# Fixing the TensorE order of seven block products, and holding a set of sums behind the last split before them

## The chip, the cores and the metric

The kernel runs on one core of one Trainium2 chip. The metric is the device time in microseconds from start to end of one execution. Matmuls run on TensorE (PE), loads of their stationary operand are shown as PEld. VectorE (DVE), ScalarE (ACT), GpSimd (POOL) and SyncE (SP, which issues most DMAs) work beside it. Each engine works off its own queue in a fixed order, and engines wait for each other by semaphores.

## The reference

One layer of a sequence model with 1024 frames and width 1024, in float32: a norm, one wide projection, three parallel mixers, a gated sum of their outputs, an output projection with a residual, and then the part that matters here:

```
u = causal_dwconv(rmsnorm(x, norm2_g[l]) @ w_up[l], ffn_conv_w[l], ffn_conv_b[l])
u_g, u_v = jnp.split(u, 2, axis=-1)
x = x + (jax.nn.silu(u_g) * u_v) @ w_down[l]
return rmsnorm(x, final_g)
```

`w_up` is 1024 x 5632, that is 44 blocks of 128 output channels, two blocks (gate and value) for each of 22 channel groups f. The convolution has three taps along the frames.

## The kernel before, in words

Activations are kept with channels on the partitions and frames along the free axis, in two halves of 512 frames. Every float32 operand is split into a rounded part and a rest ("hi" by a ScalarE cast, L99, "lo" by a VectorE subtraction, L100), and a product takes three matmuls for each 128 rows of contraction: hi by hi, hi by lo, lo by hi.

**The plain blocks.** The second norm (`norm`, L867) scales the eight row tiles of each half of the frames in place in `x2`, on VectorE (L874), and splits each into `p_hi` and `p_lo`. The first half of the frames is normalised during the output projection, the second half inside `up_end` (L895), while TensorE works on the first two blocks of `w_up`. `up_end` is a `manual_schedule` block for PE, DVE and ACT: there the instructions of the block keep their written order on each of the three engines, while instructions from outside the block may still be put between them. Groups f = 0, 1, 2 (`up_begin`, `up_end`, `up_plain`) are computed as six plain products of 48 matmuls, each into a two-bank PSUM tile `ps_g`, of which there are two. `up_conv` (L883, by `conv`, L577) reads such a tile: one ACT instruction (L581) and two taps on DVE (L585). The tile is free for another product when the second tap has read it.

**The pairs.** For f = 3 to 21, the two blocks of a group and the two halves of the frames form a 2 x 2 block product, which `pair_gemm` (L173) does with seven half-size products instead of eight, each of twelve matmuls over 512 columns. Their left operands are the weight `wa` (first block), and `s12`, `s34`, `qb`, made from both blocks in `operands` (L142) by four in-place sums on DVE (L159) and by splits. The `operands` instructions are traced with `high_priority(offset=200)`. Of the tiles `w_b` (for `qb`) and `w_s` (for `s12` and `s34`) there is room for one pair; of `wa` for two. The third sum of L159 overwrites the raw block that `qb` is split from. Their right operands are three quarters of the normalised input, b11, b21, b22, and four sums of quarters, t1 to t4, which `sums` (L206) makes once, in place in `x2`: eight DVE subtractions (L214), each followed by a split (a cast and an L100 subtraction, tile `t`).

The seven products, as written, with x and y the two banks of one `ps_g` tile, z and v banks of their own (`ps_m`):

- P1: wa by b11 into x; ACT copies x away (u0, L188)
- P2: wa by b21 into y; DVE adds y and u0 (L183, first half of the first result c)
- P3: s12 by t2, accumulated on x; ACT copies x away (u1)
- P4: s12 by t1 into z; DVE adds z to u1
- P5: s34 by t3, accumulated on x; ACT copies x away (u2); DVE adds z and u2
- P6: s34 by b22 into v; DVE adds v and u1 (second half of the first result c)
- P7: qb by t4, accumulated on x; ACT copies x (L204, second result c)

Both results then go through `up_conv`, a Silu (L919), a product (L920) and a store to DRAM (L219).

**What sets the order.** Outside `manual_schedule` blocks, a planner in the compiler orders each engine's queue ahead of time from its own estimate of durations: among what it holds to be ready it takes the instruction of the best priority, which is the earlier one in the program, where `high_priority(offset=200)` counts as 200 instructions earlier. The products of `pair_gemm` lie in no such block, nor does `sums`.

Of the kernel before, what the change touches and what calls it, by code (L numbers as in the profile page):

```python
# [9 lines left out]
F32 = mybir.dt.float32  # L10
# [3 lines left out]
ALU = mybir.AluOpType  # L14
# [8 lines left out]
HALF = 512  # L23
# [24 lines left out]
class Trunk:  # L48
# [48 lines left out]

    def split(self, hi, lo, src, eng=None):
        self.nc.scalar.copy(out=hi, in_=src)  # L99
        (eng or self.nc.vector).tensor_tensor(out=lo, in0=src, in1=hi.bitcast(F32), op=ALU.subtract)  # L100

    def weight(self, src, dst=None):
        with self.tc.high_priority(offset=200):
# [69 lines left out]
    def pair_gemm(self, pool, srcs, outs):  # L173

        nc = self.nc
        wa, s12, s34, qb = self.operands(pool, srcs)
        b11, b21, b22, t1, t2, t3, t4 = self.bs
        ps = self.pg.tile([P, T], F32, name="ps_g")
        x, y = ps[:, 0:HALF], ps[:, HALF:]
        z, v = (self.pm.tile([P, HALF], F32, name="ps_m") for _ in range(2))  # L180
        oa, ob = outs
        tmp = lambda: pool.tile([P, HALF], F32, name="u", bufs=4)
        add = lambda out, p, q: nc.vector.tensor_tensor(out=out, in0=p, in1=q, op=ALU.add)  # L183
        u = []

        def keep():
            u.append(tmp())
            nc.scalar.copy(out=u[-1], in_=x)  # L188

        self.product(wa, 0, b11, x)  # L190
        keep()
        self.product(wa, HALF, b21, y)
        add(oa[:, 0:HALF], y, u[0])
        self.product(s12, HALF, t2, x, start=False)
        keep()
        self.product(s12, 0, t1, z)
        add(u[1], z, u[1])
        self.product(s34, 0, t3, x, start=False)
        keep()
        add(ob[:, HALF:], z, u[2])  # L200
        self.product(s34, HALF, b22, v)
        add(oa[:, HALF:], v, u[1])
        self.product(qb, 0, t4, x, start=False)
        nc.scalar.copy(out=ob[:, 0:HALF], in_=x)  # L204

    def sums(self, pool, xs):  # L206

        (x11, x21), (x12, x22) = [[x[:, ks] for ks in (slice(0, KT // 2), slice(KT // 2, KT))] for x in xs]
        new = lambda: [pool.tile([P, KT // 2, HALF], F32R, name="t", align_bytes=ALIGN, bufs=8) for _ in range(2)]
        t4, t1, t2, t3 = (new() for _ in range(4))  # L210
        for to, out, p, q in ((t1, x11, x12, x11), (t3, x12, x22, x12), (t2, x22, x22, x11), (t4, x21, x21, x22)):
            for k in range(0, KT // 2, 2):
                ks = slice(k, k + 2)
                self.nc.vector.tensor_tensor(out=out[:, ks], in0=p[:, ks], in1=q[:, ks], op=ALU.subtract)  # L214
                self.split(to[0][:, ks], to[1][:, ks], out[:, ks])
        return [[[t[part][:, k] for k in range(KT // 2)] for part in range(2)] for t in (t1, t2, t3, t4)]
# [886 lines left out]
def build(tc, ins, outs, dbg=None):  # L1103
    stages = dbg or dict(hg=8, ml=4, mb=4, rest=True)
    left = dict(side="left", reuse_waits="tile")
    right = dict(side="right", reuse_waits="tile")
    with ExitStack() as ctx:
        t = Trunk(tc, ctx, ins, outs, dbg)
        t.y_dram = [outs[f"y{i}"] for i in range(3)] if dbg else [
            t.dr.tile([KT, P, T], F32, name=f"y_dram{i}") for i in range(3)]  # L1110
        t.x2_d = t.dr.tile([KT, P, T], F32, name="x2_dram")
        t.act_d = t.dr.tile([22, P, T], F32, name="act_dram")
        with tc.tile_pool(name="gp", bufs=3, **right) as t.gp:
            with tc.tile_pool(name="hp", bufs=1, **right) as hp:
                with ExitStack() as ms:
                    late = ms.enter_context(tc.tile_pool(name="late", bufs=1, **right))
                    early = lambda: Mix(ms.enter_context(tc.tile_pool(name="early", bufs=1, **right)), late)
                    mp, begun, v = t.first(hp, early)
                    t.late_consts(late)
                    t.hg_setup()  # L1120
                    for hd in range(stages["hg"]):
                        if hd and hd % 2 == 0:
                            v = t.hg_v(mp, hd // 2)
                        t.hg_head(mp, hd, v, begun if hd == 0 else None)
                        if hd == 5:
                            t.scalars(mp)
                    for hd in range(stages["ml"]):
                        t.ml_head(mp, hd)
                    for g in range(stages["mb"]):
                        t.mb_group(mp, g)  # L1130
                if not stages["rest"]:
                    return
                yp = ctx.enter_context(tc.tile_pool(name="yp", bufs=KT, **left))
                xps = ExitStack()
                xp = xps.enter_context(tc.tile_pool(name="x2", bufs=2, **left))
                br = t.branches(yp, xp)
                mixed = next(br)
            with tc.tile_pool(name="mx", bufs=KT, **right) as mxp:
                mix = [t.pair(mxp, mixed[j]) for j in range(KT - 2)]
                for _ in br:  # L1140
                    pass
                mix += [t.pair(mxp, mixed[j]) for j in range(KT - 2, KT)]
                x2 = [xp.tile([P, KT, HALF], F32, name="x2") for _ in range(2)]

                hs = [[[], []] for _ in range(4)]
                for n, part, e in itertools.product((1, 0, 2, 3), range(2), ("p_hi", "p_lo")):
                    w = yp.tile([P, T], F32R, name=e, align_bytes=ALIGN, bufs=KT)
                    hs[n][e == "p_lo"] += [w[:, 0:HALF], w[:, HALF:]]
                place = lambda part, kt, hf: hs[kt // 4 * 2 + hf][part][kt % 4]
                rhs = lambda part, kt, ts: place(part, kt, ts.start // HALF)  # L1150
                tmp = t.halves_of(lambda: t.gp.tile([P, T], F32, name="gate", bufs=3))
                src = [lambda kt, hf=hf: x2[hf][:, kt] for hf in range(2)]
                sums = lambda hf: t.norm_sums(tmp, src[hf], slice(0, HALF))

                def norm2(dg, hf):
                    t.norm(src[hf], dg, src[hf], "norm2_g",
                           lambda kt, a: t.split(place(0, kt, hf), place(1, kt, hf), a))
                t.out_proj(mix, x2, 0, range(KT))
                t.out_proj(mix, x2, 1, [0])
                dg = sums(0)  # L1160
                t.out_proj(mix, x2, 1, [1])
                norm2(dg, 0)
                t.out_proj(mix, x2, 1, range(2, KT))
            begun = t.up_begin(rhs)
            dg = sums(1)
            with tc.tile_pool(name="tp", bufs=1, **right) as tp:
                ws = t.up_end(*begun, lambda: norm2(dg, 1))
                t.up_plain(range(1, PLAIN), rhs, ws)
                t.bs = [hs[0], hs[2], hs[3]] + t.sums(tp, x2)
                xps.close()  # L1170
                with tc.tile_pool(name="a1", bufs=1, **left) as pool:
                    t.up_pairs(pool, range(PLAIN, 22))
            with tc.tile_pool(name="dn", bufs=1, **right) as pool:
                t.down(yp, pool)
# [15 lines left out]
```

## Time and profile before

| what | value |
|---|---|
| median of 3 runs | 2552.4 us (2552.34 to 2555.36) |
| profiled execution, device time | 2553.12 us |
| its span | 2551.4 us |
| PE busy | 2498.3 us, 98% of the span, 13076 matmuls |
| DVE busy | 1427.4 us, 56% |
| ACT busy | 963.0 us, 38% |
| mean granted clock of TensorE | 0.992 of full speed |

The device time of the profiled execution is 1.7 us longer than its span. Busy shares are over the whole span; a busy PE counts a pipelined matmul from its start to its modelled end (389 ns), although the next starts about 227 ns after it, so gaps have to be read from the starts. Times in rows are microseconds from the start of the span.

### The profile page before, as it was taken

Reading aid. Unit: us, or ns where it says so; the run is one execution under the profiler, and the core shown is the slowest. Engines: PE = TensorE matmul, PEld = TensorE weight load, DVE = VectorE, ACT = ScalarE, POOL = GpSimd, SP = SyncE. Lnnn points to the kernel's source line nnn. Section 1 sums busy time; section 2 is a strip of 40 time slices with the busy share of each in tenths; the row PEclk is TensorE's granted clock in tenths of the full one; section 3 lists DMA queues with packets and bytes.
Section 4 is the critical chain, followed back from the end, with each engine's and each line's share of the span. In section 5 each row is a group of like instructions: output and inputs, shape, how many; then the busy total and the mean of one; then the engine's idle time right before and its main releaser. Section 6 shows DMA issues by size and latency. Waiting matters only on the chain.

```text
span 2551.4 us, 30921 instructions
## 1 busy us (share of the span) xinstructions
PE 2498.3 (98%) x13076; PEld 2135.3 (84%) x13076; DVE 1427.4 (56%) x1792; ACT 963.0 (38%) x1177; POOL 42.1 (2%) x73
## 2 busy tenths in 40 slices
PE   8999999999999999999999999999989999999998
PEld 7898989898899899899888888888777777778886
DVE  6576767773344466675412223234766777775445
ACT  5444444553343346355312112122334444451212
POOL 1000000000000000000000000000000000000000
PEclk8999999999999999999999999999999999999999
DMA  4111111111121122212312213115211222244321
GB/s 148 34 42 42 42 42 38 58 50 58 67 75 66 43 83 83 76 54 86 124 50 93 73 48 111 48 63 172 95 66 58 85 88 75 75 142 152 111 75 66
DMA packets 56363, 195.06 MB, mean 76 GB/s; under 512 B 6536, under 2 KB 7176, under 8 KB 56224
## 3 DMA queue, kind: packets, MB, share of 16 engines
q1 hardware_dynamic: 48320, 164.77, 19.5%
q0 software_dynamic: 7904, 28.32, 2.8%
q8 instruction: 103, 1.69, 0.3%
q14 instruction: 36, 0.29, 0.0%
HBM read 160.45 MB, written 32.60 MB: 76 GB/s over the span
## 4 chain that ended last, share of the span: by engine, by line
PE 94%; DVE 3%; ACT 1%; DMA 1%; issue 1%; DVEq 0%; SPq 0%; ACTq 0%
PE ps_g L136 54%; PE ps_g L170 10%; PE ps_g L251 10%; PE ps_m L136 5%; PE ps_m L170 4%; PE ps_m L444 3%; PE ps_m L776 1%; PE ps_m L251 1%; PE ps_m L453 1%; PE ps_m L687 1%; PE ps_m L658 1%; PE ps_m L463 1%; PE ps_m L416 0%; PE ps_m L638 0%; PE ps_m L660 0%
## 5 line engine op out<-in xcount | busy, mean ns | idle before, releaser
L136 PE MATMUL ps_g<-h,w_hi 128*128 128x512 f32 x2592 | 721.6, 396 | 3.5 <-DVE h L100 2.0
L136 PEld LDWEIGHTS ps_g<-h,w_hi 128*128 128x128 f32 x2592 | 484.4, 188 | 103.4 <-ACT h L99 3.1
L99 ACT CAST w_hi<-w_raw 128x1024 fp32r<-128x1024 f32 x190 | 198.6, 1046 | 845.0 <-PE ps_g L136 722.6
L100 DVE TENSOR_TENSOR w_lo<-w_raw,w_hi 128x1024 fp32r<-128x1024 f32 x190 | 232.5, 1224 | 335.7 <-ACT w_hi L99 335.3
L136 PE MATMUL ps_g<-h,w_lo 128*128 128x512 f32 x1296 | 411.0, 394 | 0.0
L136 PEld LDWEIGHTS ps_g<-h,w_lo 128*128 128x128 f32 x1296 | 243.7, 188 | 50.4
L251 PE MATMUL ps_g<-w_hi,h 128*128 128x256 f32 x1408 | 261.1, 284 | 0.0
L136 PE MATMUL ps_g<-p_hi,w_hi 128*128 128x512 f32 x768 | 241.9, 393 | 8.7 <-DVE gate L585 6.6
L136 PE MATMUL ps_g<-p_lo,w_hi 128*128 128x512 f32 x768 | 241.3, 392 | 2.8 <-DVE p_lo L100 2.5
L136 PE MATMUL ps_g<-p_hi,w_lo 128*128 128x512 f32 x768 | 240.7, 391 | 0.0
L251 PEld LDWEIGHTS ps_g<-w_hi,h 128*128 128x128 f32 x1408 | 221.3, 192 | 0.6
L251 PE MATMUL ps_g<-w_lo,h 128*128 128x256 f32 x704 | 200.1, 284 | 0.0
L136 PEld LDWEIGHTS ps_g<-p_hi,w_hi 128*128 128x128 f32 x768 | 145.1, 189 | 40.6 <-ACT t L99 7.0
L136 PEld LDWEIGHTS ps_g<-p_lo,w_hi 128*128 128x128 f32 x768 | 145.2, 189 | 35.3 <-DVE p_lo L100 4.8
L136 PEld LDWEIGHTS ps_g<-p_hi,w_lo 128*128 128x128 f32 x768 | 145.1, 189 | 30.1
L251 PEld LDWEIGHTS ps_g<-w_lo,h 128*128 128x128 f32 x704 | 134.9, 192 | 0.5
L170 PE MATMUL ps_g<-t,w_s 128*128 128x512 f32 x456 | 113.3, 391 | 1.9 <-DVE w_s L100 1.2
L585 DVE SCALAR_TENSOR_TENSOR gate<-c,c_vec,gate 128x1023 f32<-128x1023 f32 x76 | 97.2, 1279 | 25.0 <-ACT gate L581 25.0
L170 PEld LDWEIGHTS ps_g<-t,w_s 128*128 128x128 f32 x456 | 85.4, 188 | 21.2 <-DVE w_s L100 1.6
L962 DVE TENSOR_TENSOR x<-ps_g,x 128x1024 f32<-128x1024 f32 x40 | 49.0, 1225 | 91.3 <-PE ps_g L136 86.9
L840 DVE TENSOR_TENSOR gate<-ps_g,gate 128x1024 f32<-128x1024 f32 x16 | 19.6, 1225 | 123.4 <-PE ps_g L136 123.4
L99 ACT CAST p_hi<-w_raw 128x1024 fp32r<-128x1024 f32 x48 | 50.1, 1048 | 92.3 <-DMA w_raw<-act_dram 33.6
(292 smaller groups left out, 3531.5 us busy)
## 6 DMA issues: line engine op xcount, KB each, us to landing
w_raw<-w_up SPq DMA_DIRECT2D x44, 512.0 KB, 3.5
w_raw<-w_hg SPq DMA_DIRECT2D x24, 512.0 KB, 3.4
w_raw<-w_v SPq DMA_DIRECT2D x24, 512.0 KB, 3.4
ta<-rows SPq DMA_DIRECT2D x24, 512.0 KB, 4.3
w_raw<-w_gate SPq DMA_DIRECT2D x24, 512.0 KB, 3.4
w_raw<-w_br SPq DMA_DIRECT2D x24, 512.0 KB, 3.5
w_raw<-y_dram SPq DMA_DIRECT2D x24, 512.0 KB, 3.5
act_dram<-gate POOLq DMA_DIRECT2D x22, 512.0 KB, 3.2
```

Of the source, the lines that this page charges most:

```text
L99: self.nc.scalar.copy(out=hi, in_=src)
L100: (eng or self.nc.vector).tensor_tensor(out=lo, in0=src, in1=hi.bitcast(F32), op=ALU.subtract)
L136: self.nc.tensor.matmul(out=out, lhsT=w[:, ks], rhs=rhs(part, kt, ts), start=kt == 0 and w is hi and part == 0, stop=kt == kts - 1 and w i ...
L170: self.nc.tensor.matmul(out=out, lhsT=w[x][:, ks], rhs=b[y][k], start=start and k == i == 0, stop=stop and k == 3 and i == 2, skip_group_c ...
L251: self.nc.tensor.matmul(out=out, lhsT=self.h[hf][part][:, 4 * i + k, o:o + P], rhs=w[:, ks], start=start and k == 0 and w is hi and part = ...
L444: nc.tensor.matmul(out=pa[0:m, c], lhsT=z[:, c * P:c * P + m], rhs=part(1)[:, c], start=True, stop=True)
L453: nc.tensor.matmul(out=pa[:, j], lhsT=c3(k)[:, c + j], rhs=qs[:, c + j], start=True, stop=True)
L463: nc.tensor.matmul(out=po[:, j], lhsT=A[:, c], rhs=v[:, c, vs], start=True, stop=c == 0)
L585: nc.vector.scalar_tensor_tensor(out=out[:, a:ts.stop], in0=ps[:, a - d:ts.stop - d], scalar=w(d), in1=out[:, a:ts.stop], op0=ALU.mult, op ...
L658: nc.tensor.matmul(out=po, lhsT=A[:, c], rhs=v[:, c], start=True, stop=c == 0)
L687: nc.tensor.transpose(out=pt[:, j], in_=src(4 * hf + j), identity=self.ident)
L962: nc.vector.tensor_tensor(out=x2[j], in0=ps, in1=x2[j], op=ALU.add)
```

## The change

Two edits. In `pair_gemm`, the seven products and what stands between them move into a new method `seven`, called inside a `manual_schedule` block for TensorE alone: the 84 matmuls of a pair keep their written order, P1 to P7, on TensorE. The other engines, and the order of one pair's matmuls against another pair's, stay with the planner. And `sums` is traced under `issue_after`, which queues each of its DVE instructions behind the last `lo` subtraction of the second norm on that engine's queue; it adds no wait.

```diff
     def split(self, hi, lo, src, eng=None):
         self.nc.scalar.copy(out=hi, in_=src)
-        (eng or self.nc.vector).tensor_tensor(out=lo, in0=src, in1=hi.bitcast(F32), op=ALU.subtract)
+        return (eng or self.nc.vector).tensor_tensor(out=lo, in0=src, in1=hi.bitcast(F32), op=ALU.subtract)
...
+        with self.tc.manual_schedule(engines={mybir.EngineType.PE}):
+            self.seven(wa, s12, s34, qb, (x, y, z, v), u, keep, add, oa, ob)
+        nc.scalar.copy(out=ob[:, 0:HALF], in_=x)
+
+    def seven(self, wa, s12, s34, qb, banks, u, keep, add, oa, ob):
+        b11, b21, b22, t1, t2, t3, t4 = self.bs
+        x, y, z, v = banks
         self.product(wa, 0, b11, x)
         keep()
         self.product(wa, HALF, b21, y)
...
         self.product(qb, 0, t4, x, start=False)
-        nc.scalar.copy(out=ob[:, 0:HALF], in_=x)
...
+                done = []
+
                 def norm2(dg, hf):
                     t.norm(src[hf], dg, src[hf], "norm2_g",
-                           lambda kt, a: t.split(place(0, kt, hf), place(1, kt, hf), a))
+                           lambda kt, a: done.append(t.split(place(0, kt, hf), place(1, kt, hf), a)))
...
-                t.bs = [hs[0], hs[2], hs[3]] + t.sums(tp, x2)
+                with tc.issue_after(done[-1].ins):
+                    t.bs = [hs[0], hs[2], hs[3]] + t.sums(tp, x2)
```

## Rows read from the trace of the kernel before

**Rows 1.** The page's chain of work that ended last, by engine.
```profile
PE 94%; DVE 3%; ACT 1%; DMA 1%; issue 1%; DVEq 0%; SPq 0%; ACTq 0%
```

**Rows 2.** Windows: PE, PEld, DVE, ACT, POOL busy, granted clock, DMA share, GB/s.
```profile
2000.00:2100.00 100.00, 96.63 (x421) 78.31 (x420) 76.57 (x86) 46.23 (x55) 2.65 (x5) 1.00 0.23 78
```

**Rows 3.** Waits of PE, 1830 to 2300: us in total, times, longest.
```profile
PE ps_g L170 <- ACT u L188: 14.6, 20, 1.8
PE ps_g L136 <- DVE gate L585: 6.6, 1, 6.6
PE ps_g L136 <- DVE p_lo L100: 2.5, 2, 1.9
```

**Rows 4.** Timeline of PE over one pair: start, us, line, tiles, count, idle before.
```profile
1988.04 3.01 PE L170 MATMUL ps_g<-t,w_b 128*128 128x512 f32 x12 [0.68 <-ACT u L188]
1990.89 0.39 PE L170 MATMUL ps_g<-p_hi,w_hi 128*128 128x512 f32 x1
...
1993.61 0.39 PE L170 MATMUL ps_g<-p_hi,w_hi 128*128 128x512 f32 x1
...
1996.33 0.61 PE L170 MATMUL ps_g<-t,w_s 128*128 128x512 f32 x2
...
1997.69 2.47 PE L170 MATMUL ps_g<-t,w_s 128*128 128x512 f32 x10
...
2004.53 2.88 PE L170 MATMUL ps_g<-t,w_s 128*128 128x512 f32 x12
2008.09 3.02 PE L170 MATMUL ps_g<-t,w_b 128*128 128x512 f32 x12 [0.68 <-ACT u L188]
```

**Rows 5.** Line 170, 1994.53 to 1994.60: the semaphore instruction on PE's queue.
```profile
L170 PEldq EVENT_SEMAPHORE  x1: 51/51/51, 1994.5 to 1994.5; - x1
```

**Rows 6.** Timeline of DVE over the same pair.
```profile
1987.05 1.28 DVE L585 SCALAR_TENSOR_TENSOR gate<-c,c_vec,gate 128x1023 f32<-128x1023 f32 x1 [1.32 <-ACT gate L581]
...
1991.83 0.69 DVE L100 TENSOR_TENSOR w_b<-w_raw,w_b 128x512 fp32r<-128x512 f32 x1 [1.70 <-ACT w_b L99]
1992.55 0.69 DVE L159 TENSOR_TENSOR w_raw<-w_raw 128x512 f32<-128x512 f32 x1
1993.81 0.69 DVE L183 TENSOR_TENSOR c<-ps_g,u 128x512 f32<-128x512 f32 x1 [0.56 <-PE ps_g L170]
...
1995.01 1.28 DVE L585 SCALAR_TENSOR_TENSOR gate<-c,c_vec,gate 128x1023 f32<-128x1023 f32 x1
1996.21 2.35 DVE L100 TENSOR_TENSOR w_s<-w_raw,w_s 128x1024 fp32r<-128x1024 f32 x2
```

**Rows 7.** Timeline of ACT over the same pair.
```profile
1987.40 1.07 ACT L188 COPY u<-ps_g 128x512 f32<-128x512 f32 x2 [0.38 <-PE ps_g L170]
...
1991.19 0.60 ACT L99 CAST w_b<-w_raw 128x512 fp32r<-128x512 f32 x1
...
1993.46 1.03 ACT L99 CAST w_s<-w_raw 128x1024 fp32r<-128x1024 f32 x1
```

**Rows 8.** Timeline of PE in the last part of the second norm.
```profile
1838.17 0.50 PE L136 MATMUL ps_g<-p_lo,w_hi 128*128 128x512 f32 x1 [1.90 <-DVE p_lo L100]
...
1860.72 1.19 PE L136 MATMUL ps_g<-p_hi,w_hi 128*128 128x512 f32 x2 [6.56 <-DVE gate L585]
```

**Rows 9.** Timeline of DVE in the same stretch.
```profile
1836.30 1.22 DVE L214 TENSOR_TENSOR x<-x,x 128x1024 f32<-128x1024 f32 x1
1837.44 0.68 DVE L100 TENSOR_TENSOR p_lo<-x,p_hi 128x512 fp32r<-128x512 f32 x1
...
1850.62 0.69 DVE L100 TENSOR_TENSOR p_lo<-x,p_hi 128x512 fp32r<-128x512 f32 x1
...
1856.89 0.75 DVE L585 SCALAR_TENSOR_TENSOR gate<-ps_g,c_vec,gate 128x512 f32<-128x512 f32 x1
...
1859.82 0.75 DVE L585 SCALAR_TENSOR_TENSOR gate<-ps_g,c_vec,gate 128x512 f32<-128x512 f32 x1
```

**Rows 10.** The window behind that wait, with PE's granted clock.
```profile
1861.00:1867.00 6.00, 6.00 (x16) 4.66 (x16) 6.00 (x6) 1.99 (x2) 0.00 (x0) 0.54 0.28 87
```

More of the change, by code (lines that the diff above doesn't have):

```diff
@@ L176, in pair_gemm @@
         wa, s12, s34, qb = self.operands(pool, srcs)
-        b11, b21, b22, t1, t2, t3, t4 = self.bs
         ps = self.pg.tile([P, T], F32, name="ps_g")
```

## The prediction, made before the changed kernel ran

> **What bounds the kernel now.** I read the page's chain first: TensorE holds 94% of what ended last [rows 1], so a change pays only where it closes a gap between matmuls or opens one. The windows of the pair stage show PE busy for 96.63 of 100 us at clock 1.00, with DVE at 76.57 and ACT at 46.23 [rows 2]. The list of PE's waits then names the gaps: 20 times an ACT copy of u, and once each, in the stretch ahead of the pairs, the conv taps (6.6 us) and, 2.5 us in all, the lo parts of the norm [rows 3]. Last, the timelines. Over one pair [rows 4] they show the order that the planner chose: P7 of pair A (from 1988.04), P2 of pair B (1990.89), P1 of pair C (1993.61), two matmuls of P3 of B (1996.33), five of P4 and P6 as filling, the ten others of P3 (1997.69), P4 and P6, P5 (2004.53), a wait for u2, and P7 (2008.09). That the first twelve of 1990.89 are P2 is read from DVE, which adds y and u0 at 1993.81, right behind them [rows 6].
>
> **Part 1, the order of the seven products: what goes.** A pair takes 2008.09 - 1988.04 = 20.05 us [rows 4]. Matmuls follow each other by (1993.61 - 1990.89) / 12 = 0.227 us, so 84 of them take 19.04 us, and 1.0 us a pair is lost. Nearly all of it lies behind P5: its twelve matmuls from 2004.53 would let P7 start at 2007.25, and it starts at 2008.09, 0.84 later, with about 0.1 more in the first steps after the wait (its twelve take 3.02 us where P5's take 2.88). I count 0.95 a wait. In the written order P6, 12 x 0.227 = 2.72 us, stands between P5 and P7, and the copy, about 0.6 us long (1.07 for two) [rows 7], lies beneath it. The wait goes, 20 times [rows 3]: 19.0 us at most from this alone.
>
> **What may come: two more reads of the same tile.** At 1994.5 PE's queue works off a semaphore instruction [rows 5], directly after DVE's addition of y and u0 ends (1993.81 + 0.69 = 1994.50) [rows 6]. P3 writes x, and the addition reads y, the other bank of the same tile; I read this as P3 waiting for that addition, and take it that P2 waits in the same way for the copy u0. Today P1 of the next pair hides the first, and u0 was copied before P7 (the second of the two copies at 1987.40) [rows 7]. If a pair ran by itself in the written order, each place would cost about what the copy costs today, 0.95, and 0.99 + 0.11 = 1.1 for the addition (its end against P2's last start plus a step, 1994.60 - 1993.61). The edit does not tie one pair to the next, so P1 of the next pair, 2.72 us, can stand there as it does today. I take nothing for these two; the other end is 2.05 us a pair.
>
> By the Trainium skill, "PSUM — Partial Sum Buffer", section "PSUM bank collisions raise a hardware error", a semaphore has to guard PSUM by bank and quadrant, so a reader of y need not hold up a writer of x, and these two places would cost nothing in any order. The semaphore behind the addition says otherwise here. By the rule the gain would be 19.0 us whatever the planner interleaves; by the row it needs the next pair as cover.
>
> **The chain behind P7.** There is room for one pair's `w_b`, so after P7 of A come, one after another: the cast of `w_b` (1991.19), its lo (1991.83), the third sum of L159 (1992.55), the cast of `s12` (1993.46), its lo (1996.21, the first of two that take 2.35 together, so done at about 1997.4) [rows 6, 7]. Counted from 1990.89, the lo is there after 6.5 us. The third matmul of P3 needs it. Today it starts after 6.8 us, because five matmuls of P4 and P6 were put ahead. In the written order it comes after 24 + 2 matmuls, 5.9 us. So with DVE's queue unchanged PE would wait 0.6 us, and with 0.1 each for the semaphore and the restart lose 0.85 of the 0.95 again. Two things in the chain can give way: DVE waits 0.56 us for y ahead of the addition, and then runs a conv tap of 1.2 us ahead of the lo [rows 6]. Without the tap it is there after 5.3 us, with neither after 4.8, and nothing is lost. But the written order also moves P6 behind P5, and with it the first result's two taps (today before P7, 1987.05) [rows 6] into this very window: 2 x 1.2 = 2.4 us more on DVE.
>
> I choose no loss, since these operand instructions carry priority over the taps and addition, and a tap that starts before them costs at most its 1.2 us: a lo due at 4.8, plus one such, is 6.0, all but on time. The ends are a gain of 0.95 and a loss of 1.45 a pair (below). The first pair has no cover yet and may pay at the two reads what it saves, so I count 18 of the 20 waits: 18 x 0.95 = 17.1 us.
>
> **Part 2, the sums behind the last split.** They remain 16 DVE instructions, with their ACT casts. Today six of them, four L214 and two t, lie between 1836.30 and the last p_lo at 1850.62 [rows 9]; one takes 1837.44 - 1836.30 = 1.14 us of the queue. The first delays the first p_lo, on which PE sits idle for 1.90 us [rows 8]. Moving them brings the last p_lo forward by 6 x 1.14 = 6.8 us. The lo waits of 2.5 us [rows 3] go, but that alone ends nothing: PE next needs a free `ps_g`, which the second tap frees, and waits 6.56 us for it, until 1860.72 [rows 8]. The first tap stands at 1856.89, five sum instructions behind the last p_lo, the second at 1859.82, two further on [rows 9]. If the planner leaves five sums ahead of the first tap again, both taps and PE's restart move 6.8 us forward. If it places the taps by PE's progress, the six merely go elsewhere ahead of them, and the gain is 0. At best all goes: 6.6 + 2.5, and the half-speed stretch after the wait, 16 matmuls in 6 us at clock 0.54 [rows 10] where 6 / 0.227 = 26 fit, 10 x 0.227 = 2.3 us: 11.4. I take 6.8, the reading by the row of the tap. The lo of the next weight and the Silu lie behind the taps as now; the sums' first reader is a product of the first pair, behind two whole plain groups, so that later sums cost nothing.
>
> **The sum.** 17.1 + 6.8 = 23.9 us off the profiled execution's 2553.1: 2529.2. The median lies 0.7 below that execution: **2528.5 us**.
>
> **Rivals.** (1) The wait moves to the lo of s12, at equal price. For it: the 6.5 against 5.9 us above, and a DVE at 77% whose queue is fixed ahead. Against: the order of DVE is planned anew. Part 1 then gives (0.95 - 0.85) x 19 = 2 us, with part 2 2543.6; without part 2, 2550, no change.
>
> The Trainium skill's "Perfetto Trace Analysis", section "Optimization Strategy", says that a gap that repeats can mean too little memory for the next tile. Here the repeating gap ends with a copy, yet `w_b` for one pair is what this rival hangs on; by that rule, order alone would not remove it.
>
> (2) The other side: the chain behind P7 becomes the bound. Three taps of the two results stand ahead of the lo on DVE. From the end of w_b's cast, 0.9 us behind P7, DVE then works without a break, its short instructions (0.69 busy, less the overlap of some 0.08 that 1.22 busy and 1.14 apart show [rows 9]) 0.6 each: three taps 3.6, w_b lo 0.6, L159 twice 1.2, the addition 0.6, the lo 1.2: 8.1 us. PE waits 8.1 - 5.9 + 0.2 = 2.4 a pair in place of 0.95; 19 x 1.45 = 27.5 us more. With part 2 that is 2573, without 2580. It decides from the point where the lo comes later than 5.9 + 0.95 - 0.2 = 6.65 us behind P7. For it: 2.4 us move into a window that has some 0.1 to spare; against: the priority of the operands. Pairs without cover would come out at the same: 2.05 - 0.95 = 1.1 a pair, 21 us.
>
> (3) The planner keeps what matters as it was, taps and filling: 2552.
>
> **How the numbers follow.** Forecast 0.44; rival 1 0.20; rival 2 0.30; rival 3 0.06. The forecast's own range is 2517 (19.0 + 11.4, and the odd longer waits) to 2537 (15, no part 2). Under 0.2%, 5 us, nothing can be told from no change. Faster: 0.44 and 0.11 of rival 1, 0.55. Same: 0.09 of rival 1, 0.04 of rival 3, 0.02 of a mild rival 2, 0.15. Slower 0.30. The range that holds 8 in 10 has to reach rival 2: 2518 to 2574.
>
> **What would show it.** Right: no wait for u in the list; 84 matmuls from P7 to P7 in 19.0 to 19.2 us; P1 of the next pair between P2 and P3; the lo of s12 under 5.9 us behind P7; no L214 ahead of the last p_lo, and PE's restart near 1854. Wrong in part 1: waits for DVE `w_s` (rivals 1, 2), or for ACT u at P2 and DVE c at P3 (no cover). Wrong in part 2: the taps still near 1857 and a wait for them longer than 6.6 us.

## The result, and the profile after

The changed kernel takes **2583.91 us** (median of 4 runs, 2583.8 to 2587.7) where the kernel before took 2552.56 beside it: ratio **1.0124, 95% interval 1.0106 to 1.0141**, 31 us slower. The forecast was 2528.5 us. It lies 11 us above what the second rival gave (2573) and 10 above the end of the range.

The page's chain by engine, where TensorE has fallen from 94% [rows 1] and DVE risen from 3%:

```profile
PE 88%; DVE 8%; ACT 1%; issue 1%; DMA 1%; DVEq 0%; SPq 0%; ACTq 0%
```

The same window as [rows 2], and two windows of 4 us; columns as there. DVE and ACT do less in the same time, because the pairs come more slowly. The clock column, which was 1.00 in every window of the pairs before, falls to 0.97, and to 0.57 and 0.59 in the short windows:

```profile
2000.00:2100.00 100.00, 92.45 (x390) 74.90 (x389) 66.70 (x76) 41.73 (x51) 2.66 (x5) 0.97 0.23 76
...
1976.00:1980.00 4.00, 4.00 (x12) 3.11 (x12) 1.23 (x2) 1.38 (x2) 0.53 (x1) 0.57 0.91 282
2020.00:2024.00 4.00, 4.00 (x12) 3.15 (x11) 1.38 (x2) 1.43 (x2) 0.53 (x1) 0.59 0.92 267
```

PE's waits, 1820 to 2340, against [rows 3]. The 20 waits for a copy of u are gone but for one; in their place stand 18 for the lo of `s12`, 17 of them of 1.89 us and the last pair's of 3.4:

```profile
PE ps_g L170 <- DVE w_s L100: 35.5, 18, 3.4
PE ps_g L136 <- DVE gate L590: 6.8, 1, 6.8
PE ps_g L170 <- DVE w_lo L100: 2.6, 1, 2.6
...
PE ps_g L136 <- DVE p_lo L100: 0.8, 1, 0.8
PE ps_g L170 <- ACT u L187: 0.7, 1, 0.7
```

PE over one pair (P7, P2's first, P1 of the next pair's first, P3, P3 again), answering [rows 4]:

```profile
2052.61 2.88 PE L170 MATMUL ps_g<-t,w_b 128*128 128x512 f32 x12
2055.33 0.39 PE L170 MATMUL ps_g<-p_hi,w_hi 128*128 128x512 f32 x1
...
2058.05 0.39 PE L170 MATMUL ps_g<-p_hi,w_hi 128*128 128x512 f32 x1
...
2060.77 0.62 PE L170 MATMUL ps_g<-t,w_s 128*128 128x512 f32 x2
...
2063.27 2.56 PE L170 MATMUL ps_g<-t,w_s 128*128 128x512 f32 x10 [1.89 <-DVE w_s L100]
```

P7 follows P6 with no wait, and P1 of the next pair stands between P2 and P3, both as forecast. The third matmul of P3 starts at 2063.27, 2.5 us behind the first. DVE and then ACT in the same pair show why (against [rows 6, 7]):

```profile
2054.82 1.28 DVE L590 SCALAR_TENSOR_TENSOR gate<-c,c_vec,gate 128x1023 f32<-128x1023 f32 x1 [1.31 <-ACT gate L586]
2056.02 0.68 DVE L100 TENSOR_TENSOR w_b<-w_raw,w_b 128x512 fp32r<-128x512 f32 x1
2056.62 1.27 DVE L590 SCALAR_TENSOR_TENSOR gate<-c,c_vec,gate 128x1022 f32<-128x1022 f32 x1
2057.81 0.68 DVE L159 TENSOR_TENSOR w_raw<-w_raw 128x512 f32<-128x512 f32 x1
2058.42 1.27 DVE L590 SCALAR_TENSOR_TENSOR gate<-c,c_vec,gate 128x1023 f32<-128x1023 f32 x1
2059.61 0.68 DVE L182 TENSOR_TENSOR c<-ps_g,u 128x512 f32<-128x512 f32 x1
2060.21 0.68 DVE L159 TENSOR_TENSOR w_raw<-w_raw 128x512 f32<-128x512 f32 x1
2060.81 1.27 DVE L590 SCALAR_TENSOR_TENSOR gate<-c,c_vec,gate 128x1022 f32<-128x1022 f32 x1
2062.00 2.35 DVE L100 TENSOR_TENSOR w_s<-w_raw,w_s 128x1024 fp32r<-128x1024 f32 x2
```

```profile
2055.30 0.62 ACT L99 CAST w_b<-w_raw 128x512 fp32r<-128x512 f32 x1 [0.52 <-PE ps_g L170]
...
2057.93 1.06 ACT L924 ACTIVATE gate<-gate 128x1024 f32<-128x1024 f32 x1 [0.24 <-DVE gate L590]
2058.90 1.04 ACT L99 CAST w_s<-w_raw 128x1024 fp32r<-128x1024 f32 x1
```

All four taps stand ahead of the lo of `s12`. The second holds up the third sum of L159 by its 1.2 us, and on ACT a Silu (L924) holds up the cast by another 0.4 (the sum ends at 2058.49, the cast starts at 2058.90), so that the cast ends only at 2059.94; and then an addition, a sum and the last tap go first, so that the lo starts at 2062.00. It is the first of the two instructions in that row and ends near 2063.2, 7.9 us behind P7's end at 2055.33.

The starts of consecutive matmuls give the account of the pair stage (first matmul of the first pair to the first plain product behind the last pair; the 1608 steps between would take 364.2 us at 0.2265 each). "Waits" is the sum of gaps beyond a step that are over 0.3 us, "half speed" that of steps of 0.35 to 0.53 us:

| kernel | stage, us | waits | half speed |
|---|---|---|---|
| before | 388.6 | 20.6 | 0 |
| both edits | 424.4 | 44.0 | 12.3 |

23.4 us are longer waits and 12.3 us are matmuls at the 1.2 GHz level, 0.43 us apart, about eight of them in seven of the pairs and at the stage's end. Part 2 gives back 5.2: the first pair starts at 1901.82 where it started at 1907.07 (1901.95 with the sums alone, `e2` below). 35.8 - 5.2 = 30.6 is the difference of the spans (2582.0 - 2551.4).

### The profile page after: what moved, and what is told of

Its sections match the earlier page's. It is cut to its first block, busy times and chain, and to the rows that moved or that the text cites. A ratio compares the mean times of both kernels' runs of the same rounds, so it can differ in the third digit from the quotient of the medians.

```text
span 2582.0 us, 30945 instructions
## 1 busy us (share of the span) xinstructions
PE 2508.1 (97%) x13076; PEld 2146.0 (83%) x13076; DVE 1424.5 (55%) x1792; ACT 964.1 (37%) x1177; POOL 42.1 (2%) x73
## 4 chain that ended last, share of the span: by engine, by line
PE 88%; DVE 8%; ACT 1%; issue 1%; DMA 1%; DVEq 0%; SPq 0%; ACTq 0%
PE ps_g L136 53%; PE ps_g L256 9%; PE ps_m L136 5%; PE ps_g L170 4%; PE ps_m L170 4%; DVE gate L590 3%; PE ps_m L449 3%; PE ps_m L781 1%; PE ps_m L256 1%; DVE c L182 1%; ACT gate L586 1%; PE ps_m L458 1%; DVE w_s L100 1%; PE ps_m L692 1%; PE ps_m L663 1%
## 5 line engine op out<-in xcount | busy, mean ns | idle before, releaser
L170 PE MATMUL ps_g<-t,w_s 128*128 128x512 f32 x456 | 124.6, 420 | 38.1 <-DVE w_s L100 35.5
```

The source lines that it names most:

```text
L170: self.nc.tensor.matmul(out=out, lhsT=w[x][:, ks], rhs=b[y][k], start=start and k == i == 0, stop=stop and k == 3 and i == 2, skip_group_c ...
```

## The experiments

Each was timed in several executions beside the kernel before, unless said otherwise. The line numbers in their rows can differ by one from those of the changed kernel.

**Each part alone.** `e1` drops the `issue_after`, `e2` the `manual_schedule`.

> Only the written order of the seven products; the sums stay where they were. Theory (the whole loss lies in the pairs: each waits some 2.1 us for the lo of s12, and half of them run eight matmuls at the lower clock): the pairs cost what they cost with both edits, 22.05 us each, and the 5.3 us that the sums brought are lacking: 2589 us. Rival (moving the sums puts DVE's queue out of step, and the order itself gains what was forecast): 2535 us, with 19.1 us a pair and no wait for w_s.

> Only the sums behind the last split; the planner is free to order the products. Theory: the wait for the second tap ends some 4.4 us earlier and the pairs begin 5.3 us earlier, nothing else changes: 2547 us, 20.05 us a pair, a wait for the copy u2 in each pair. Rival (the moved sums are what disturbs the pairs): 2575 us or more. Rival (the sums' gain appears only where the pairs wait less): 2552 us.

```diff
 # e1
-                with tc.issue_after(done[-1].ins):
-                    t.bs = ...
+                t.bs = ...
 # e2
-        with self.tc.manual_schedule(engines={mybir.EngineType.PE}):
+        if True:
             self.seven(...)
```

The order alone: **2585.48 us, ratio 1.0128 (1.0113 to 1.0144)**. The sums alone: **2548.68, 0.9983 (0.9974 to 0.9993)**. So the loss is the order's, and the sums do what was meant, at a little over half the forecast's size. With the order, the sums bring 1.6 us, not 3.9, a difference within the spread of these runs (2583.8 to 2587.7 and 2584.25 to 2587.92). The two profiled executions show where such a difference can come from: the order alone starts its pairs 4.0 us later than both edits, but its stage takes 420.7 us with waits of 40.2, against 424.4 and 44.0.

**Cutting the chain: room for two pairs' `w_b`.**

> Both edits, and room for the w_b of two pairs; for the memory the copies u have three buffers in place of four. The cast of w_b no longer waits for P7, so the third sum and the cast of s12 can be done long before. Theory (the serial chain behind P7 is what makes the lo late): no wait for w_s, no half-speed stretch, 19.1 to 19.3 us a pair: 2583.9 - 18 x 2.85 = 2533 us. Rival A (DVE puts three or four taps ahead of the lo whatever the chain): the wait stays at 2 us, 2575 to 2585 us. Rival B (the third matmul of P3 really waits for the addition of y and u0 on the same tile): the same 2575 to 2585 us, with the wait then named for DVE's addition. Rival C (the clock falls without the waits): the waits go, the half-speed stretches stay, 2583.9 - 18 x 2.1 = 2546 us.

```diff
-            qb = new("w_b", HALF, 2)
+            qb = new("w_b", HALF, 4)       # and w_b without align_bytes, for space
...
-        tmp = lambda: pool.tile([P, HALF], F32, name="u", bufs=4)
+        tmp = lambda: pool.tile([P, HALF], F32, name="u", bufs=3)
```

**2530.76 us, ratio 0.9913 (0.9898 to 0.9927)**: 53 us less than with both edits alone, 22 less than before. No wait for `w_s` is left in the list, and a window of 100 us holds the 442 matmuls that 0.2265 us each would allow:

```profile
2000.00:2100.00 100.00, 100.00 (x442) 82.68 (x441) 80.67 (x91) 50.51 (x60) 2.66 (x5) 1.00 0.25 85
```

DVE is busier than ever (80.67 of 100), so it was not its total load that made the lo late. The lo of `s12` is now made while P5 of the pair before runs, some 11 us ahead of its use, and its cast waits for P4, the last product to read the one room of `s12`, instead of for what hangs on P7. ACT, DVE and PE:

```profile
2030.18 1.05 ACT L99 CAST w_s<-w_raw 128x1024 fp32r<-128x1024 f32 x1 [1.91 <-PE ps_m L171]
...
2031.27 1.23 DVE L100 TENSOR_TENSOR w_s<-w_raw,w_s 128x1024 fp32r<-128x1024 f32 x1
...
2030.21 2.88 PE L171 MATMUL ps_g<-t,w_s 128*128 128x512 f32 x12
```

Rivals A and C are out. B, the reads of the same tile, is out as the cause here; what those reads cost uncovered is measured below.

**Keeping the chain, moving taps behind the lo.** With one pair's room for `w_b`, the operands of the next pair are traced ahead of the convolutions, and DVE takes the last two taps (`e5`) or the last one (`e6`) behind the lo. No run has the earlier tracing alone; that the taps count is read from the step between one and two.

> Both edits, one pair's room for w_b, and the two taps of the second result are queued on DVE behind the lo of s12 of the next pair (for that the operands of the next pair are traced ahead of the convolutions). Theory (four taps ahead of the lo on DVE make it late, 4 x 1.2 us): two of them leave, the lo comes 2.4 us earlier, at 5.5 to 5.9 us behind P7, where 26 matmuls take 5.9: waits under 0.3 us, 19.1 to 19.5 us a pair, 2583.9 - 18 x 2.7 = 2535 us (2530 to 2545). Rival A (the serial chain of casts alone makes it late, the taps only fill its gaps): the wait stays at 1.5 us or more, 2570 us or more. Rival B (the moved taps make something else late, the lo of s34 or the addition that shares their tile c): no wait for the lo of s12 in P3, but one at P5 or at the addition, 2560 us or more.

> Both edits, one pair's room for w_b, and only the very last of the four taps queued behind the lo of s12 (a dose between both edits and the run with two taps behind it). Theory: the lo comes one tap, 1.2 us, earlier, PE waits 2.05 - 1.2 = 0.85 us a pair with 0.1 at the restart; a wait of that size did not bring the lower clock in the kernel before, so the half-speed stretches of every second pair, 0.8 us a pair, go altogether: 20.0 us a pair, 2583.9 - 18 x 2.05 = 2547 us. Rival A (the half-speed stretches do not hang on the size of the wait): 20.8 us a pair, 2562 us. Rival B (the chain alone sets the lo, all taps fill gaps): 2580 us or more.

```diff
-            self.split(*s12, raw[1])
+            self.lo = self.split(*s12, raw[1])
...
+            ops = get(f + 1) if f + 1 in fs else None
             us = []
             for n, c in zip(ns, cs):
...
-                self.up_conv(us[-1], c, n)
+                with self.tc.issue_after(self.lo.ins) if ops and n % 2 else nullcontext():
+                    self.up_conv(us[-1], c, n)     # e6: round the last tap alone
```

Two taps: **2532.85 us, 0.9921 (0.9906 to 0.9936)**; one tap: **2549.10, 0.9987 (0.9978 to 0.9996)**. One tap of 1.2 us behind the lo takes the wait from 2.05 to 0.86 us a pair, two take it away. DVE's order with two taps moved, and, for one, PE's wait list and a window over the pairs:

```profile
2022.29 0.68 DVE L159 TENSOR_TENSOR w_raw<-w_raw 128x512 f32<-128x512 f32 x1
2022.89 0.68 DVE L182 TENSOR_TENSOR c<-ps_g,u 128x512 f32<-128x512 f32 x1
2023.49 0.68 DVE L159 TENSOR_TENSOR w_raw<-w_raw 128x512 f32<-128x512 f32 x1
2024.44 1.23 DVE L100 TENSOR_TENSOR w_s<-w_raw,w_s 128x1024 fp32r<-128x1024 f32 x1 [0.27 <-ACT w_s L99]
2025.58 1.28 DVE L590 SCALAR_TENSOR_TENSOR gate<-c,c_vec,gate 128x1023 f32<-128x1023 f32 x1
```

```profile
PE ps_g L170 <- DVE w_s L100: 13.9, 18, 2.1
...
1930.00:2230.00 300.00, 289.53 (x1259) 234.85 (x1259) 227.19 (x255) 140.35 (x165) 7.99 (x15) 1.00 0.23 79
```

In the first, DVE itself waits 0.27 us for the cast: the chain is now the limit, and it ends in time. So the chain and the taps each suffice as a lever; it is their sum that was too long. The second answers a question of the clock: with 17 waits of 0.86 (the 18th, the last pair's, is longer) the granted clock is 1.00 from 1930 to 2230, and half speed falls from 12.3 to 2.0 us, all of it at the stage's end. Rival A of that run is out.

**The chain with no taps at all**, timed in a single execution; the kernel leaves out the two taps of each convolution of the pairs and keeps its first step.

> Both edits, one pair's room for w_b, and the four taps of each pair left out, so that DVE has nothing but operands, additions and the product of gate and value between P7 and the lo of s12 (the convolution of the pairs is cut to its first step). Theory (the chain by itself is what the prediction said, done 4.8 to 5.3 us behind P7, and the taps are the rest): no wait for w_s, 19.06 to 19.3 us a pair, the stage as with two taps moved, 2530 us. Rival (the chain by itself is already later than 5.9 us): a wait of 0.5 us or more in each pair, 2545 us or more.

```diff
-                self.up_conv(us[-1], c, n)
+                self.nc.scalar.activation(out=us[-1], in_=c, func=AF.Identity, ...)
```

2541.83 us: between the theory and the rival. 17 waits of 0.48 us (0.75 lost in each with the restart) and a longer one at the end stay. DVE and ACT behind P7, which ended at 2002.7:

```profile
2004.52 0.69 DVE L159 TENSOR_TENSOR w_raw<-w_raw 128x512 f32<-128x512 f32 x1
2005.62 0.69 DVE L182 TENSOR_TENSOR c<-ps_g,u 128x512 f32<-128x512 f32 x1 [0.41 <-PE ps_g L170]
2006.23 0.68 DVE L159 TENSOR_TENSOR w_raw<-w_raw 128x512 f32<-128x512 f32 x1
2006.83 1.22 DVE L925 TENSOR_TENSOR gate<-gate 128x1024 f32<-128x1024 f32 x1
2007.97 1.22 DVE L100 TENSOR_TENSOR w_s<-w_raw,w_s 128x1024 fp32r<-128x1024 f32 x1
...
2003.16 0.60 ACT L99 CAST w_b<-w_raw 128x512 fp32r<-128x512 f32 x1
...
2005.43 1.03 ACT L99 CAST w_s<-w_raw 128x1024 fp32r<-128x1024 f32 x1
```

ACT casts `w_b` 0.5 us behind P7's end, behind a Silu, and `s12` from 2005.43 to 2006.46. So the chain, with this delay in it, would let the lo end at about 2006.5 + 1.2 = 2007.7, 5.0 us behind P7: the prediction's 4.8 holds. But without taps the planner puts the product of gate and value there, and the lo ends 6.4 us behind P7. What stands ahead of the operands changes; that something of lower priority does, stays.

**The room without the order.**

> The sums behind the last split and room for the w_b of two pairs (u in three buffers), but no order for the products. Theory (the room for w_b is what the pairs lack, with or without the order): freed of the chain, the planner's queue has ten matmuls of P4 and two of P6 between P5 and P7, enough for the copy u2, but only two of P4 between P3 and P5, 0.45 us where the copy u1 needs 0.84, so that some 0.4 + 0.1 us a pair stay: 19.5 us a pair, 2530.8 + 18 x 0.5 = 2540 us, 2531 if that wait does not show. Rival (the order is what takes the wait for u2 away, the room only makes the order bearable): 20.05 us a pair, 2548 us as with the sums alone.

**2551.41 us, 0.9996 (0.9987 to 1.0006)**: the theory, 2540, missed by 11 us, and the rival's 2548 is nearer, though by another mechanism than it named: the wait for u2 is gone, and this stands in its place.

```profile
PE ps_m L171 <- ACT w_s L99: 17.4, 19, 1.7
```

It costs 1.07 us a pair and 0.11 at the restart, behind P3. ACT and PE there:

```profile
1998.35 1.04 ACT L99 CAST w_s<-w_raw 128x1024 fp32r<-128x1024 f32 x1 [6.66 <-PE ps_g L171]
1999.30 0.58 ACT L188 COPY u<-ps_g 128x512 f32<-128x512 f32 x1
...
1995.66 2.88 PE L171 MATMUL ps_g<-t,w_s 128*128 128x512 f32 x12
1999.45 0.74 PE L171 MATMUL ps_m<-t,w_s 128*128 128x512 f32 x2 [0.91 <-ACT w_s L99]
```

PE restarts as the cast ends (1998.35 + 1.04 = 1999.39), before the copy of u does (1999.88), so the cast is what it waits for. The cast itself waits for P3's end. This reads as the cast of the next pair's `s12`, which has room for one pair and P3 as its last reader, and the two matmuls as the first two of the next pair's P4, which the planner put there; more room for `w_s` was not tried. For the loss it is enough that order alone costs 33 us, room alone gains nothing beside the sums alone, and both together gain 22.

The Trainium skill's "Perfetto Trace Analysis", section "Optimization Strategy", says that a gap repeating over a stretch can mean too little memory for the next tile. The gap of the changed kernel was of that kind (`w_b`, 53 us); of the one of the kernel before this is not shown, since with the room alone that gap went, another took its place, and the time stayed as it was.

**The reads of the same tile, uncovered.** The `manual_schedule` is put round all pairs, on top of the room for two `w_b`, so P1 of the next pair cannot stand between P2 and P3.

> Both edits, room for two w_b, and the written order held on PE over all pairs, so that P1 of the next pair comes behind P7 of this one and no longer stands between P2 and P3. Theory (the reads of the same tile cost what the prediction put on them when nothing covers them): P2 waits for the copy u0, 0.95 us, P3 for the addition of y and u0, 1.1 us: 19.06 + 2.05 = 21.1 us a pair, 2530.8 + 18 x 2.05 = 2568 us, up to 14 us more if the lower clock comes with it. Rival (P2 and P3 touch another bank than the one that is read, and wait for nothing): 2531 us.

```diff
-                    t.up_pairs(pool, range(PLAIN, 22))
+                    with tc.manual_schedule(engines={mybir.EngineType.PE}):
+                        t.up_pairs(pool, range(PLAIN, 22))
```

**2568.42 us, 1.0062 (1.0047 to 1.0077)**, the forecast to the microsecond. P2 waits for u0 (first row), P3 for the addition (second):

```profile
2011.41 0.50 PE L171 MATMUL ps_g<-p_hi,w_hi 128*128 128x512 f32 x1 [0.68 <-ACT u L188]
...
2015.28 0.96 PE L171 MATMUL ps_g<-t,w_s 128*128 128x512 f32 x3 [0.85 <-DVE c L183]
```

In this program a writer of one bank waits for the reader of the other bank of the same tile. The Trainium skill's "PSUM — Partial Sum Buffer", section "PSUM bank collisions raise a hardware error", asks for a guard by bank and quadrant only; here the two share the tile and not the bank, and the runs do not show that the hardware needs the wait.

**Sums later still**, on top of the room for two `w_b`: behind the second tap of the first plain block (`e8`), and behind the last tap of group f = 1 (`e9`).

> Both edits with room for two w_b, and the sums not behind the last lo of the norm but behind the second tap of the first plain block's second half, the tap that PE waits for. Theory (nine sum instructions on DVE ahead of the second tap keep PE idle for 6.8 us and bring seven half-speed matmuls): the tap comes within 1.5 us of its product's end, PE waits 1 us at most: 2530.8 - 6 - 1.7 = 2523 us. Rival (ACT's first conv step or the next weight sets PE's restart, the sums only fill DVE): 2529 us or more.

> Both edits with room for two w_b, the sums behind the last tap of the second plain group (f = 1). Theory (what the run with the sums behind one tap lost again was the same thing one tap later: sums ahead of a tap that PE waits for): the two waits of 6.8 and 3.0 us both go, no half-speed stretch ahead of f = 2, and seven sum instructions ahead of the first tap of f = 2, 8 us, cost at most 2 us there: 2528.8 - 3.5 - 1.8 + 2 = 2525 us (2523 to 2529). Rival (wherever the sums stand in the plain groups, the third wait is as long as the first was, or the first pair waits for its operands): 2529 us or more.

```diff
-            self.up_conv(us[0], ps[0], 0, HALVES[1])
+            self.tap = self.up_conv(us[0], ps[0], 0, HALVES[1])     # e8; e9 keeps the last tap of f = 1
...
-                with tc.issue_after(done[-1].ins):
+                with tc.issue_after(t.tap.ins):
```

**2528.76 us, 0.9907 (0.9893 to 0.9922)**, and **2530.39, 0.9913 (0.9896 to 0.9929)**, beside 2530.76 without. Both times are 5 to 6 us above what was expected. The wait of 6.8 us shrinks to 0.5 in both and a shorter one comes where the sums now meet a tap; in `e8` 26 us later, ahead of f = 2 (first two rows), in `e9` ahead of the first pair (third row):

```profile
1850.45 0.70 PE L136 MATMUL ps_g<-p_hi,w_hi 128*128 128x512 f32 x2 [0.50 <-DVE gate L591]
...
1876.79 0.70 PE L136 MATMUL ps_g<-p_hi,w_hi 128*128 128x512 f32 x2 [2.97 <-DVE gate L591]
```

```profile
1897.32 0.47 PE L171 MATMUL ps_g<-p_hi,w_hi 128*128 128x512 f32 x1 [3.94 <-DVE gate L591]
```

In `e8` the first pair starts only 1.0 us earlier than without (1900.27 against 1901.24). In `e9` the stage of the pairs begins at 1897.32 where it begins at 1901.24 with the sums behind the last lo, and takes 375.3 us instead of 370.9. The lowest median is that of `e8`, 24 us under the kernel before; its 2.0 us under the run without are not clear of the noise, for the intervals of the ratios overlap (0.9893 to 0.9922 and 0.9898 to 0.9927).

## Why the prediction was wrong

**The step that failed** is "I choose no loss, since these operand instructions carry priority over the taps and addition". All that led up to it held: the wait for u2 went, P1 of the next pair covered the two reads, the chain without taps needs 5.0 us where 4.8 were worked out (`e11`), and 5.9 is when PE is there. Priority did not keep the window clear. The trace after has four taps ahead of the lo, two of them ahead of a sum on which the lo hangs, and even with no tap in the program a product of gate and value went first. The queue is written ahead of time from estimated durations; a reading that fits the traces is that an operand not yet ready by the estimate does not hold DVE free, and whatever is ready takes the slot. The planner's own estimates were not seen, so this stays a reading. The prediction had the price of the other choice in rival 2: lo at 8.1 us behind P7 (7.9 measured), PE losing 2.4 us a pair (2.05 and 0.11 at the restart). It also had the reason to weigh it more: it said itself that 2.4 us of taps move into a window with 0.1 to spare.

**What no case had** is the clock, 12.3 us. Rival 2's 2573 with 12.3 for the clock, and part 2 smaller by 1.6, and 23.4 of longer waits where 27.5 were counted, is 2573 + 12.3 + 1.6 - 4.1 = 2582.8, against 2583.9.

**The gain of 17.1 us** for part 1 was sound as a size: where the chain is cut, the stage is 17.7 us shorter than before (388.6 - 370.9). It was a gain that the order could not give alone.

**Part 2** was forecast at 6.8 us. The first tap did come 6.6 us earlier, at 1850.25 where [rows 9] have 1856.89, with no sum ahead of the last p_lo. The term mis-sized is the second tap, which PE waits for: four sum instructions stand between the two taps now, where two stood before, and it came at 1855.45 instead of 1859.82, 4.4 earlier. With a shorter half-speed stretch behind it, the first pair starts 5.2 us earlier; the run with the sums alone is 3.9 us faster.

**Rival 1** named the right wait, for the lo of `s12`, at a price of 0.85 where 2.16 were paid. Rival 3 is out: the list of waits changed altogether.

**Two readings in the prediction are off** without touching its forecast. Ahead of the ten others of P3 stand four matmuls of P4 and P6, not five (1996.78 to 1997.69 is 4 x 0.227), and the terms of the 0.85 in rival 1 add up to 0.8.

## What to carry to other kernels

Fixing the order on one engine moves work into other engines' windows: before forcing it, lay the other engine's queue over the new order, instruction by instruction, and treat a priority as a wish and not as a reservation. Where the operands of a step hang on a buffer that is freed only just before the step, give that buffer a second room first; here the order gained 22 us with it and cost 33 without it. A wait that is moved out of one place by queueing work elsewhere is gone only when the queue behind it has been read to the next consumer.

## What was not expected of the hardware

In these runs the lower clock went with the length of a single wait, not with the idle time of a pair. With one wait of 1.89 us in 21.3, matmuls ran at the 1.2 GHz level in seven of seventeen pairs, the stretches beginning 0.8 to 1.5 us behind the restart and two or three pairs apart (1976, 2021, 2086, 2130, 2195, 2239, 2284). With two waits in a pair, 0.68 and 0.85 us, 3 us apart and together as long (2.08 us lost with the restarts, against 2.16), the clock stayed at 1.00 over the pairs:

```profile
1930.00:2230.00 300.00, 278.05 (x1188) 220.92 (x1189) 219.91 (x242) 131.78 (x155) 7.99 (x15) 1.00 0.22 74
```

A long wait did not always bring it: with room for two `w_b` a single one of 1.9 us at 2234 was followed by none of it. Why the 1.89 us bring it in some pairs and not in all stays open.
